# A two-layer encoder trunk in fp32: two of four weight sums made by accumulating transfers, heads turned some steps after their gating, last chunks of output blocks bank by bank

## The chip, the core and the metric

The kernel runs on one core of one Trainium2 chip. The metric is the device time of one execution in microseconds (us), of which several runs were taken and the median is given. The core's engines are named as in the profile: PE (TensorE matmul), PEld (its weight loads), DVE (VectorE), ACT (ScalarE), POOL (GpSimd) and SP (SyncE, which here only issues transfers).

## The reference

Two layers, 512 tokens, model width 2048, all in float32. Each layer normalises its input, projects it with one matrix of 7184 columns, runs two head groups on the columns, and maps the gated result back with a 2048x2048 matrix.

```python
h = rmsnorm(x, g_pre)
z = h @ w_in                                    # 2048 x 7184
gq, gk, gv, gg, ga, aq, ak, av, ag = split_columns(z)
log_a = log_sigmoid(ga @ w_alpha + b_alpha) / 16          # forget gate, rank 16
o_gla = gla_chunk_causal(gq, gk, gv, log_a)     # 4 heads, chunks of 64: S_c = a*S_(c-1) + k_dec^T v; o = q S_c
o_gla = rmsnorm(o_gla, g_gla) * silu(gg)
o_att = chunk_band_attention(aq, ak, av, rel_bias)        # 8 heads of 128, softmax over own and earlier chunks
o_att = rmsnorm(o_att, g_att) * silu(ag)
y = concatenate([o_gla, o_att]) @ w_out         # 2048 x 2048
return x + rmsnorm(y, g_post)
```

## The kernel before

**Products.** A product of two fp32 matrices is made of three matmuls in a rounded format: each operand is split into a high part (the rounded value) and a low part (what is left), and high x high, high x low and low x high are added up in PSUM. Weights are split on the chip. A job of the weight stream is one chunk of 128 partitions by 1024 fp32 (512 KB): `load` is its transfer on SP's queue (line 141, into a tile `raw` or `H`), `high` its cast on ACT (line 183, `wh`), `low` the subtraction on DVE (line 187, `wl = source - wh`). `ahead()` runs after each job and prepares loads up to five jobs ahead, `high` up to four and `low` three. The rings have four tiles `raw`, four `H`, four `wh`, three `wl` and four `sa` (streamed activations).

**Blocks.** A layer's weights are 18 blocks of 512 columns (14 of the input projection, 4 of the output projection). Two input blocks and two output blocks go through `std_gemm`: eight chunks, four PSUM banks, one for each 128 tokens, 24 matmuls of 128x512 for each chunk (line 275). The other blocks go in pairs through `fast_gemm`: a pair of blocks is made by seven half-size products P1, P5, P6, P3, P7, P2, P4 of four chunks each, 28 jobs where plain products would need 32. There are six such pairs of input blocks (`PAIRS[0]` to `PAIRS[5]`) and one of output blocks (`W23`, `end` in the code). `PAIRS[2]` and `PAIRS[3]` hold the attention's q and k and are made feature-major with matmuls of 128x256 (line 339); the rest are token-major with 128x512 (line 349). The products accumulate in two pairs of banks, X and Y, in turn.

**Weight sums.** P5, P6, P7 and P2 need sums of weight quarters. With b0 and b1 the two blocks and top and bottom their halves, P1 loads H = b0 top; P5 loads a `raw` and adds it, H += b1 top (DVE, line 176); P6 the same with b1 bottom (line 176); P7 loads b0 top again and takes raw = H - raw, which is b1 top + b1 bottom (DVE, line 180); P2 loads b0 bottom and adds it to H after the split (line 190). In `W23` the order is P2, P7, P4 and P7 adds two loaded `raw` tiles (line 178).

**Side work.** Everything else (attention heads, forget gate, recurrence, activation sums, norms) is written as Python generators in `tasks`. After each job `Pace` advances them by `rate` steps (`pump`), and so places their instructions between the jobs' instructions. A scheduler then orders each engine's instructions by priority, which follows the order of the code. The steps named below are, with the lines of the kernel before:

- `attend`, two heads a and b in the order of the string `ORDER`: scores (S, three matmuls, lines 718 to 720), transposes of the probabilities (T, 739), product with the values (P, 756), gate (G, DVE line 770 into a tile `sg`), turn (R, four transposes of `sg` on PE, line 781, then a copy on ACT and two splits).
- `forget_gate_decay`: a running sum over tokens by matmuls with a constant triangle (lines 623, 624, 626, 635) of the logarithm of the forget gate, whose high and low parts come from ACT and DVE (`split`, lines 105 and 106).
- GLA units (four for every two heads): `outer` (904, products of decayed keys and values, whose operands are split by lines 105 and 106), `states`, `read` (937), `norm`, `gate` (955), `turn` (965).
- `output_sums`: sums of output activations for `W23` (lines 497 to 506), written to memory as `oS` by POOL's queue (line 492).
- Line 1070 is the eviction of an output block's bank on DVE; line 448 the first normalisation.

PSUM has four banks for the blocks (`mm`) and four for side work (`ax`).

Of the kernel before, what the change touches and what calls it, by code (L numbers as in the profile page):

```python
# [33 lines left out]
def hybrid_trunk(  # L34
# [100 lines left out]
    class Job:  # L135
# [7 lines left out]

        def load(self):
# [7 lines left out]
            elif k == "P5":  # L152
                p["r", c] = self.fetch(rtile("raw"), b1, top)
# [5 lines left out]
            elif k == "P7":  # L159
                p["r", c] = self.fetch(rtile("raw"), b0, top)  # L160
            elif k == "P2":
                p["r", c] = self.fetch(rtile("raw"), b0, bottom)
# [5 lines left out]
        def high(self):  # L168
# [3 lines left out]
            else:  # L172
                h, r = p["H", c], p.get(("r", c))
                src = h if k in ("P1", "P5", "P6", "P4") else r
                if k in ("P5", "P6"):
# [3 lines left out]
                elif k == "P7":  # L179
                    nc.vector.tensor_tensor(out=r, in0=h, in1=r, op=ALU.subtract)  # L180
# [46 lines left out]
    tasks = []  # L227

    def pump(n):
        while n > 0 and tasks:  # L230
            try:
                next(tasks[0])
                n -= 1
            except StopIteration:
                tasks.pop(0)

    def until(cond):
        while not cond():
            assert tasks
            pump(1)  # L240

    def drain():
        while tasks:
# [325 lines left out]
    def layer(l):  # L569
# [42 lines left out]
        def forget_gate_decay():  # L612
# [20 lines left out]
            for t in range(NT):  # L633
# [13 lines left out]
                yield  # L647
                pend.append((t, la, lah, lal))
# [3 lines left out]
            yield  # L652
# [18 lines left out]
        std_gemm(l, AG1, range(NT), CO, operand_in, gate_evac(1, 1), rate=1.3)  # L671
# [33 lines left out]
        class Head:  # L705
# [90 lines left out]
            "- - aS3 aS2 aS1 aS0 aT3 bS3 aT2 aP3 bS2 aT1 aP2 bS1 aT0 aP1 bS0 aP0 aG "  # L796
            "bT3 bT2 bP3 bT1 bP2 aR bT0 bP1 bP0 bG - - - - bR"
        ).split()

        def attend(hd, qk):  # L800
            heads = {"a": Head(hd, qk, 0), "b": Head(hd + 1, qk, 1)}
            for step in ORDER:
# [10 lines left out]
                elif step[1] == "G":  # L813
                    h.gate()
                else:
                    h.turn()
                yield
            heads_done.add(hd)
# [25 lines left out]
        fast_gemm(l, PAIRS[2], qk_consume(0), rate=2, feature_major=True)  # L844
        fast_gemm(l, PAIRS[3], qk_consume(1), rate=2, feature_major=True)
# [33 lines left out]
        fast_gemm(l, PAIRS[4], kq_consume, rate=2)  # L879
# [4 lines left out]
        class Unit:  # L884
# [24 lines left out]
            def states(self):  # L909
                h, p = self.h, self.p  # L910
                self.sg = sgt([2, 256])
# [72 lines left out]
        def gla_heads(j, gvh, gvl):  # L984
# [6 lines left out]

            new(0)
# [3 lines left out]
            for k in range(5):  # L996
# [3 lines left out]
                if k < 4:  # L1000
                    units[k].read()
                    yield
# [3 lines left out]
                if k:  # L1006
                    units[k - 1].turn()
                    yield
                if k < 4:
                    units[k].norm()  # L1010
                    yield
# [183 lines left out]
```

## Time and profile before

| | |
|---|---|
| runs | 1718.1, 1722.27 and 1723.86 us, median 1722.27 |
| the profiled execution | own time 1726.13 us, span in the profile 1724.3 us |
| mean granted TensorE clock | 0.985 |
| PE busy | 1656.8 us, 96% of the span |
| DVE, ACT, POOL busy | 70%, 51%, 12% |
| transfers | 455 MB, 61.8% of 16 DMA engines' span on SP's queue and 11.8% on POOL's |

The span is what the profile covers; the own time of the same execution is 1.8 us longer. A busy share is an average over all stages. In a row of the view of waits stand the waiting engine and line, what ended the wait, the sum of such waits, their number and the longest. In a row of the view of windows stand the stretch, its length, the busy time of each engine with the number of its instructions, the granted clock (PEclk), the share of the DMA engines and GB/s. In a row of the timeline stand start, length, engine, line, operation and, in brackets, the idle time before it and what ended it.

### The profile page before, as it was taken

Reading aid. Unit: us, or ns where it says so; the run is one execution under the profiler, and the core shown is the slowest. Engines: PE = TensorE matmul, PEld = TensorE weight load, DVE = VectorE, ACT = ScalarE, POOL = GpSimd, SP = SyncE. Lnnn points to the kernel's source line nnn. Section 1 sums busy time; section 2 is a strip of 40 time slices with the busy share of each in tenths; the row PEclk is TensorE's granted clock in tenths of the full one; section 3 lists DMA queues with packets and bytes.
Section 4 is the critical chain, followed back from the end, with each engine's and each line's share of the span. In section 5 each row is a group of like instructions: output and inputs, shape, how many; then the busy total and the mean of one; then the engine's idle time right before and its main releaser. Section 6 shows DMA issues by size and latency. Waiting matters only on the chain. (4 is left out here: it accounts for less than half of the span.)

```text
span 1724.3 us, 25039 instructions
## 1 busy us (share of the span) xinstructions
PE 1656.8 (96%) x9090; PEld 1406.6 (82%) x9090; DVE 1214.7 (70%) x1547; ACT 874.0 (51%) x1444; POOL 201.9 (12%) x368
## 2 busy tenths in 40 slices
PE   7999999999999999999999999999999999999896
PEld 5888889999987876778678888899998888667784
DVE  5756877677767777476887567677777677754767
ACT  8634544455665534344584345444556555344443
POOL 0210000011202102110022000000121011021101
PEclk8999999999999999999999999999999999999999
DMA  7986886758847786596769587867686678767964
GB/s 266 344 315 229 330 297 239 278 179 292 296 146 284 245 321 240 199 351 238 244 238 385 211 314 280 314 227 260 199 308 225 205 275 281 278 220 233 371 233 168
DMA packets 143003, 455.05 MB, mean 264 GB/s; under 512 B 15444, under 2 KB 32212, under 8 KB 142880
## 3 DMA queue, kind: packets, MB, share of 16 engines
q1 hardware_dynamic: 119984, 373.76, 61.8%
q0 software_dynamic: 22176, 78.41, 11.8%
q8 instruction: 72, 1.18, 0.3%
q10 hardware_dynamic: 720, 1.28, 0.2%
q14 instruction: 51, 0.42, 0.1%
HBM read 381.28 MB, written 72.11 MB: 263 GB/s over the span
## 5 line engine op out<-in xcount | busy, mean ns | idle before, releaser
L349 PE MATMUL mm<-wh,sa 128*128 128x512 f32 x1536 | 490.0, 393 | 0.5
L183 ACT CAST wh<-raw 128x1024 fp32r<-128x1024 f32 x248 | 261.7, 1056 | 256.8 <-PE mm L349 83.6
L187 DVE TENSOR_TENSOR wl<-raw,wh 128x1024 fp32r<-128x1024 f32 x248 | 300.7, 1219 | 82.8 <-PE mm L275 25.5
L183 ACT CAST wh<-H 128x1024 fp32r<-128x1024 f32 x224 | 235.0, 1051 | 243.8 <-PE mm L349 131.8
L187 DVE TENSOR_TENSOR wl<-H,wh 128x1024 fp32r<-128x1024 f32 x224 | 273.4, 1222 | 105.4 <-PE mm L349 44.7
L349 PEld LDWEIGHTS mm<-wh,sa 128*128 128x128 f32 x1536 | 288.4, 188 | 63.0 <-issue 2.5
L349 PE MATMUL mm<-wl,sa 128*128 128x512 f32 x768 | 301.2, 392 | 7.0 <-DVE wl L187 6.9
L339 PE MATMUL mm<-sa,wh 128*128 128x256 f32 x1280 | 234.1, 284 | 0.0
L349 PE MATMUL mm<-wh,a 128*128 128x512 f32 x576 | 193.4, 406 | 7.4 <-DVE g L1070 7.4
L339 PEld LDWEIGHTS mm<-sa,wh 128*128 128x128 f32 x1280 | 199.5, 192 | 0.2
L339 PE MATMUL mm<-sa,wl 128*128 128x256 f32 x640 | 181.2, 283 | 0.0
L349 PEld LDWEIGHTS mm<-wl,sa 128*128 128x128 f32 x768 | 144.5, 188 | 38.6 <-DVE wl L187 10.2
L275 PE MATMUL mm<-wh,a 128*128 128x512 f32 x512 | 171.9, 395 | 0.1
L349 PEld LDWEIGHTS mm<-wh,a 128*128 128x128 f32 x576 | 111.8, 194 | 33.3 <-DVE g L1070 8.2
L176 DVE TENSOR_TENSOR H<-H,raw 128x1024 f32<-128x1024 f32 x112 | 136.8, 1223 | 2.8
L339 PEld LDWEIGHTS mm<-sa,wl 128*128 128x128 f32 x640 | 122.6, 192 | 0.0
L349 PE MATMUL mm<-wl,a 128*128 128x512 f32 x288 | 115.9, 402 | 0.0
L180 DVE TENSOR_TENSOR raw<-H,raw 128x1024 f32<-128x1024 f32 x48 | 58.8, 1224 | 80.2 <-DMA raw<-in_w_dram 80.1
L275 PEld LDWEIGHTS mm<-wh,a 128*128 128x128 f32 x512 | 96.2, 188 | 21.8 <-issue 1.5
L275 PE MATMUL mm<-wl,a 128*128 128x512 f32 x256 | 101.0, 395 | 2.4 <-DVE wl L187 2.4
L339 PE MATMUL mm<-a,wh 128*128 128x256 f32 x512 | 96.1, 288 | 0.0
L727 POOL TENSOR_SCALAR sm<-sm 128x1 f32<-128x1 f32 x64 | 31.8, 497 | 539.3 <-DVE sm L723 529.4
(191 smaller groups left out, 2415.6 us busy)
## 6 DMA issues: line engine op xcount, KB each, us to landing
raw<-in_w_dram SPq DMA_DIRECT2D x312, 512.0 KB, 5.2
sa<-S SPq DMA_DIRECT2D x192, 512.0 KB, 4.8
H<-in_w_dram SPq DMA_DIRECT2D x56, 512.0 KB, 5.4
sa<-A SPq DMA_DIRECT2D x48, 512.0 KB, 6.1
S<-g POOLq DMA_DIRECT2D x32, 512.0 KB, 7.6
oS<-g POOLq DMA_DIRECT2D x32, 512.0 KB, 7.2
sa<-oS SPq DMA_DIRECT2D x32, 512.0 KB, 4.7
sg<-t POOLq DMA_DIRECT2D x32, 256.0 KB, 5.6
```

What stands on the lines that cost most here:

```text
L176: nc.vector.tensor_tensor(out=h, in0=h, in1=r, op=ALU.add)
L180: nc.vector.tensor_tensor(out=r, in0=h, in1=r, op=ALU.subtract)
L183: last_cast[0] = nc.scalar.copy(self.wh, src).ins
L187: nc.vector.tensor_tensor(out=self.wl, in0=self.src, in1=self.wh.bitcast(F32), op=ALU.subtract)
L275: nc.tensor.matmul(pss[o], a[:, part, t], rhs[:, kk, :], start=(i == 0 and kk == 0 and m == 0), stop=(i == n - 1 and kk == 1 and m == 2),)
L339: nc.tensor.matmul(dst, lhs[:, kk, f], a[:, part, tok], start=(fresh and kk == 0 and m == 0 and ft % 2 == 0), stop=(c == 3 and kk == 1 and ...
L349: nc.tensor.matmul(out_ps[t], a[:, part, tok], rhs[:, kk, :], start=(fresh and kk == 0 and m == 0), stop=(c == 3 and kk == 1 and m == 2), ...
L727: nc.gpsimd.tensor_scalar(out=nmx, in0=mx, scalar1=-1.0, scalar2=None, op0=ALU.mult)
```

## The change

**Sums by transfers.** P5 no longer loads a `raw` tile on SP's queue and adds it on DVE: POOL issues a transfer that adds b1 top from memory to the tile H (`add`, line 145 of the kernel after). P7 of the six input pairs is built in the same way: b1 top is added to the `raw` tile of P6, which holds b1 bottom. P6's sum, P2's sum and P7 of `W23` stay on DVE. Per layer these are 28 and 24 transfers, so 104 in all that move from SP to POOL, and 104 DVE instructions of 128x1024 that fall away (56 of line 176, all 48 of line 180). The bytes read from memory are the same. PE and ACT execute the same instructions.

**Turns later.** A list `delayed` holds functions with a count of steps. A head's turn is put there with 8 steps when its gate is written, a GLA unit's turn with 5. Some empty steps in `ORDER`, in the forget gate and ahead of the GLA units go in or out, and the rates 2 and 1.8 become 2.1 and 1.7. The GLA units' `sg` tiles alternate between two rings.

**Last chunks bank by bank.** `std_gemm` has had an argument `lag`: the last `lag` chunks are done for one bank after the other instead of all banks for each chunk. The second input block (AG1) and the second output block now have lag=2, the first output block lag=1, which with one chunk leaves the order of matmuls as it was.

```diff
+        def add(self, tile_, blk, c):
+            nc.gpsimd.dma_start(tile_, w[self.l, blk, c].rearrange("p (k n) -> p k n", k=2), accum_op=ALU.add)
...
             elif k == "P5":
-                p["r", c] = self.fetch(rtile("raw"), b1, top)
+                self.add(p["H", c], b1, top)
...
             elif k == "P7":
-                p["r", c] = self.fetch(rtile("raw"), b0, top)
+                self.add(p["r", c], b1, top)
...
-                if k in ("P5", "P6"):
+                if k == "P6":
                     nc.vector.tensor_tensor(out=h, in0=h, in1=r, op=ALU.add)
                 elif k == "P7" and ("r2", c) in p:
                     nc.vector.tensor_tensor(out=r, in0=r, in1=p["r2", c], op=ALU.add)
-                elif k == "P7":
-                    nc.vector.tensor_tensor(out=r, in0=h, in1=r, op=ALU.subtract)
...
     def pump(n):
-        while n > 0 and tasks:
-            try:
-                next(tasks[0])
-                n -= 1
-            except StopIteration:
-                tasks.pop(0)
+        while n > 0 and (tasks or delayed):
+            for entry in list(delayed):
+                entry[0] -= 1
+                if entry[0] <= 0:
+                    delayed.remove(entry)
+                    entry[1]()
+            while tasks:
+                try:
+                    next(tasks[0])
+                    break
+                except StopIteration:
+                    tasks.pop(0)
+            n -= 1
...
-        std_gemm(l, AG1, range(NT), CO, operand_in, gate_evac(1, 1), rate=1.3)
+        std_gemm(l, AG1, range(NT), CO, operand_in, gate_evac(1, 1), rate=1.3, lag=2)
...
-            "- - aS3 aS2 aS1 aS0 aT3 bS3 aT2 aP3 bS2 aT1 aP2 bS1 aT0 aP1 bS0 aP0 aG "
+            "aS3 aS2 aS1 aS0 aT3 bS3 aT2 aP3 bS2 aT1 aP2 bS1 aT0 aP1 bS0 aP0 - aG "
...
-                elif step[1] == "G":
+                else:
                     h.gate()
-                else:
-                    h.turn()
+                    delayed.append([8, lambda h=h: turn(h)])
...
-        fast_gemm(l, PAIRS[2], qk_consume(0), rate=2, feature_major=True)
+        fast_gemm(l, PAIRS[2], qk_consume(0), rate=2.1, feature_major=True)
...
                     units[k].gate()
+                delayed.append([5, units[k].turn])
...
-        std_gemm(l, NB_IN, range(NT), OO, operand_out, out_evac(0), rate=1.8)
+        std_gemm(l, NB_IN, range(NT), OO, operand_out, out_evac(0), rate=1.7, lag=1)
...
-        std_gemm(l, NB_IN + 1, range(NT), OO, operand_out, out_evac(1), rate=0.8)
+        std_gemm(l, NB_IN + 1, range(NT), OO, operand_out, out_evac(1), rate=0.8, lag=2)
```

Three places show how the instructions move. The first is PE's order in layer 0 at the first scores of `PAIRS[2]`, in the first chunks of product P2 (`a_48`, `a_56`, `a_64` are the activations of its chunks 0, 1 and 2; `mm` and `ax` are PSUM tiles, `g_496` to `g_499` and `g_472` to `g_475` the heads' q and k). Before:

```order
L339 MATMUL mm_2396<-a_48_351,wl_3020 128x256
L718 MATMUL ax_3151<-g_498_2925,g_496_2923 128x256
L719 MATMUL ax_3151<-g_499_2926,g_496_2923 128x256
L720 MATMUL ax_3151<-g_498_2925,g_497_2924 128x256
L339 MATMUL mm_2395<-a_56_390,wh_3023 128x256 x2
```

After:

```order
L348 MATMUL mm_2363<-a_56_390,wl_3003 128x256
L729 MATMUL ax_3133<-g_474_2877,g_472_2875 128x256
L730 MATMUL ax_3133<-g_475_2878,g_472_2875 128x256
L731 MATMUL ax_3133<-g_474_2877,g_473_2876 128x256
L348 MATMUL mm_2362<-a_64_423,wh_3006 128x256 x2
```

The scores stood ahead of chunk 1 (`a_56`) of the product and now stand behind it, one job later.

The second is DVE's order at the start of `W23` in layer 0, where the banks of the last plain output block are evicted (`g8`, `g11`, `g14`, `g15`, from the four `mm` tiles) while the first chunks of `W23` are split. Before, with the tiles' numbers:

```order
L187 TENSOR_TENSOR wl_1477_7459<-H_1464_7370,wh_1469_7413 128x1024
L176 TENSOR_TENSOR H_1464_7370<-H_1464_7370,raw_1490_7542 128x1024
L106 TENSOR_TENSOR g2_1480_7466<-t2_1474_7420,g2_1480_7466 128x512
L106 TENSOR_TENSOR g3_1481_7477<-t2_1472_7418,g3_1481_7477 128x512
L187 TENSOR_TENSOR wl_1482_7499<-H_1470_7415,wh_1478_7461 128x1024
L176 TENSOR_TENSOR H_1470_7415<-H_1470_7415,raw_1501_7574 128x1024
L1070 TENSOR_TENSOR g8_1403_7111<-mm_1428_7179,t2_1427_7177 128x512
L1070 TENSOR_TENSOR g11_1406_7123<-mm_1429_7180,t2_1427_7177 128x512
L1070 TENSOR_TENSOR g14_1409_7135<-mm_1430_7181,t2_1427_7177 128x512
L187 TENSOR_TENSOR wl_1488_7538<-H_1479_7463,wh_1483_7501 128x1024
L176 TENSOR_TENSOR H_1479_7463<-H_1479_7463,raw_1505_7595 128x1024
L1070 TENSOR_TENSOR g15_1415_7153<-mm_1431_7182,t2_1427_7177 128x512
```

After:

```order
L188 TENSOR_TENSOR wl_1429_7363<-H_1416_7274,wh_1421_7317 128x1024
L106 TENSOR_TENSOR g2_1432_7370<-t2_1426_7324,g2_1432_7370 128x512
L106 TENSOR_TENSOR g3_1433_7381<-t2_1424_7322,g3_1433_7381 128x512
L1088 TENSOR_TENSOR g8_1352_7003<-mm_1380_7083,t2_1379_7081 128x512
L1088 TENSOR_TENSOR g11_1355_7015<-mm_1381_7084,t2_1379_7081 128x512
L1088 TENSOR_TENSOR g14_1361_7039<-mm_1382_7085,t2_1379_7081 128x512
L188 TENSOR_TENSOR wl_1438_7438<-H_1422_7319,wh_1430_7365 128x1024
L188 TENSOR_TENSOR wl_1439_7440<-H_1431_7367,wh_1437_7436 128x1024
L1088 TENSOR_TENSOR g15_1367_7057<-mm_1383_7086,t2_1379_7081 128x512
L188 TENSOR_TENSOR wl_1450_7472<-H_1440_7442,wh_1441_7444 128x1024
```

Two additions into H and the splits of chunks 0 and 1 stood ahead of the first eviction; now only the split of chunk 0 does, and the first three evictions stand ahead of the splits of chunks 1 to 3.

The third is POOL's order at the same place, which is new (`H_7274` is the tile of P5's chunk 0, `H_7319`, `H_7367` and `H_7442` those of its chunks 1 to 3; an `oS` is one sum of output activations):

```order
L501 DMA oS_127<-g_1427_7342 128x1024
L501 DMA oS_135<-g_1428_7353 128x1024
L145 DMA H_7274<-in_w_dram 128x1024
L501 DMA oS_131<-g_1432_7370 128x1024
L501 DMA oS_139<-g_1433_7381 128x1024
L145 DMA H_7319<-in_w_dram 128x1024
L145 DMA H_7367<-in_w_dram 128x1024
L145 DMA H_7442<-in_w_dram 128x1024
```

The sums of `W23`'s P5, which stood on DVE, now stand in POOL's queue behind the writes of the output sums, and each of these waits for its split on DVE.

48 lines of the change are left out of this document (28 added, 20 removed).

## The prediction

> **What bounds the kernel now.** I read the page's totals first, then the waits of PE, the timeline around the longest of them, and stretches of the windows view, which give the granted clock and the load of the DMA engines.
>
> ```profile
> span 1724.3 us, 25039 instructions
> PE 1656.8 (96%) x9090; PEld 1406.6 (82%) x9090; DVE 1214.7 (70%) x1547; ACT 874.0 (51%) x1444; POOL 201.9 (12%) x368
> PEclk8999999999999999999999999999999999999999
> ```
>
> PE is the bound: it is idle for 1724.3 - 1656.8 = 67.5 us, and the change leaves its instructions alone. So the time can only come from that idle time, from the clock after it, or from new waits. Which of PE's waits the change touches is in the view of waits; all but the first come once or twice in either layer, so the sums are over both.
>
> ```profile
> PE mm L349 <- DVE wl L187: 7.9, 7, 2.2
> PE mm L349 <- DVE g L1070: 7.4, 2, 3.8
> PE ax L904 <- ACT g L105: 5.2, 2, 3.2
> PE ax L718 <- ACT g L105: 3.9, 2, 2.0
> PE ax L781 <- DVE sg L770: 3.2, 2, 1.7
> PE ax L965 <- DVE sg L955: 2.5, 4, 0.7
> PE ax L965 <- issue: 1.2, 2, 0.6
> PE ax L623 <- ACT t L105: 2.1, 2, 1.1
> PE ax L624 <- DVE t L106: 1.2, 2, 0.6
> PE ax L904 <- DVE g L106: 1.0, 2, 0.5
> ```
>
> A wait has a second price. The timeline shows four of them, and the windows what clock was granted behind them (PEclk is the third number from the end).
>
> ```profile
> 335.89 0.91 PE L718 MATMUL ax<-g,g 128*128 128x512 f32 x2 [1.93 <-ACT g L105]
> 532.91 0.30 PE L781 MATMUL ax<-cst,sg 128*128 128x128 f32 x1 [1.72 <-DVE sg L770]
> 638.91 0.39 PE L904 MATMUL ax<-g,g 64*128 64x256 f32 x2 [3.16 <-ACT g L105]
> 776.47 0.79 PE L349 MATMUL mm<-wh,a 128*128 128x512 f32 x1 [3.61 <-DVE g L1070]
> ```
>
> ```profile
> core 0: us, PE busy (x) PEld busy (x) DVE busy (x) ACT busy (x) POOL busy (x), PEclk, DMA share, GB/s
> 100.00:150.00 50.00, 50.00 (x222) 41.39 (x222) 29.05 (x25) 19.82 (x23) 2.78 (x5) 1.00 0.66 234
> 155.00:231.00 76.00, 75.93 (x336) 62.56 (x335) 56.64 (x51) 38.33 (x43) 4.31 (x8) 1.00 0.82 302
> 231.00:307.00 76.00, 75.85 (x467) 68.28 (x466) 54.34 (x50) 32.72 (x35) 0.00 (x0) 1.00 0.76 271
> 336.20:339.60 3.40, 3.40 (x14) 3.12 (x13) 2.71 (x6) 1.21 (x2) 0.45 (x2) 0.50 0.79 301
> 476.10:479.50 3.40, 3.40 (x10) 2.62 (x10) 2.66 (x3) 0.78 (x2) 0.00 (x0) 0.50 0.00 0
> 640.00:643.40 3.40, 3.40 (x15) 2.39 (x13) 3.22 (x6) 0.41 (x1) 0.00 (x0) 0.51 0.34 122
> 776.50:779.90 3.40, 3.40 (x8) 2.72 (x9) 3.37 (x4) 0.00 (x0) 0.00 (x0) 0.50 1.01 406
> 1189.50:1192.90 3.40, 3.40 (x14) 3.20 (x14) 2.09 (x5) 1.33 (x4) 0.45 (x2) 0.50 0.77 295
> 1329.50:1332.80 3.30, 3.30 (x9) 2.60 (x8) 2.22 (x3) 0.45 (x2) 0.00 (x0) 0.50 0.00 0
> 1493.30:1496.70 3.40, 3.40 (x13) 1.87 (x12) 3.12 (x6) 0.00 (x0) 0.00 (x0) 0.50 0.58 204
> 1629.90:1633.20 3.30, 3.30 (x9) 2.61 (x8) 3.27 (x5) 0.00 (x0) 0.00 (x0) 0.50 0.99 384
> 533.20:536.60 3.40, 3.40 (x18) 2.75 (x17) 3.23 (x7) 1.88 (x4) 1.07 (x2) 1.00 0.64 228
> ```
>
> At full clock a 128x512 matmul takes 50 / 222 = 0.225 us. In 776.5 to 779.9 PE counts as busy but runs 8 of them, which are 1.8 us of work in 3.4 us: the stretch costs 1.6 us. There are four of them in either layer, behind the scores, the decay sums, GLA's outer products and the start of W23. Behind the head turn's wait of 1.72 us the clock stayed at 1.00, behind the scores' 1.93 us it fell to 0.50.
>
> The Trainium skill, "TensorE: Matmul & The Clock Gate", section "Why this matters for your kernels", asks for no PE-idle gaps over about 3 us, since one window of idle drops the clock. The trace differs: 1.93 us was enough. By the rule only the stalls of 3.16 us and more would carry a stretch, three as far as the rows tell, and the saving below would be 3 x 1.6 = 4.8 us in place of 12.8 us; I go by the rows.
>
> **The change, part by part.** *Later steps and last chunks.* The pairs of 28 jobs in the windows took 76 us, so a job is 2.71 us.
>
> - Scores: one job later, 2.71 us against a wait of 1.93 us; gone, 3.9 us in both layers. Nothing stands between them and the product but matmuls that are ready.
> - Decay sums: two to four empty steps more, at about two steps a job, so 2.7 to 5.4 us against 1.1 and 0.6 us; gone, 2.1 + 1.2 = 3.3 us.
> - Head turns: 8 steps behind the gate are 4 jobs, 10 us, against 1.7 us. The heads of the last pair end in a burst (the code runs steps until they are done, whatever the rate), where I leave 0.5 us; 2.7 of 3.2 us.
> - GLA outer products: four empty steps ahead, 5.4 us against 3.2 + 0.5 us; gone, 5.2 + 1.0 = 6.2 us.
> - GLA turns: all but a layer's last two are covered. In the new order these stand back to back behind the last read with 12 matmuls (2.7 us) between, while norm, POOL's power and the gate run in a row. New wait between 0 and what these turns wait now, (2.5 + 1.2) / 2 = 1.9 us a layer; I take 1.3, nearer to the old, because the chain is the old one; 3.7 - 2.6 = 1.1 us.
> - Start of W23: the wait of 3.61 us is for evictions, and DVE did other things ahead of them:
>
> ```profile
> 770.99 1.23 DVE L176 TENSOR_TENSOR H<-H,raw 128x1024 f32<-128x1024 f32 x1
> 774.59 1.22 DVE L176 TENSOR_TENSOR H<-H,raw 128x1024 f32<-128x1024 f32 x1
> 775.73 1.88 DVE L1070 TENSOR_TENSOR g<-mm,t 128x512 f32<-128x512 f32 x3
> ```
>
> The two additions (2.45 us) go, and with two chunks for each bank the first bank ends three times 6 x 0.225 = 1.35 us, 4.1 us, earlier before the end. Both together are more than 3.61 us; but chunk 7's split is needed 4.1 us earlier, too. I leave 0.8 us a layer (bounds 0 and 2); 7.4 - 1.6 = 5.8 us.
>
> These are 3.9 + 3.3 + 2.7 + 6.2 + 1.1 + 5.8 = 23.0 us. With the stalls of scores, decay, outer and W23's start go eight stretches at half clock, 8 x 1.6 = 12.8 us. If the splits were late at these places for another reason, this cover would be gone and the 12.8 us with it. The first output block's lag of one chunk costs and brings nothing, since its matmuls keep their order.
>
> *Sums by transfers.* The rows for the work that goes and for what is nearest to the new transfers:
>
> ```profile
> L176 DVE TENSOR_TENSOR H<-H,raw 128x1024 f32<-128x1024 f32 x112 | 136.8, 1223 | 2.8
> L180 DVE TENSOR_TENSOR raw<-H,raw 128x1024 f32<-128x1024 f32 x48 | 58.8, 1224 | 80.2 <-DMA raw<-in_w_dram 80.1
> L183 ACT CAST wh<-raw 128x1024 fp32r<-128x1024 f32 x248 | 261.7, 1056 | 256.8 <-PE mm L349 83.6
> raw<-in_w_dram SPq DMA_DIRECT2D x312, 512.0 KB, 5.2
> S<-g POOLq DMA_DIRECT2D x32, 512.0 KB, 7.6
> L492 POOL DMA_DIRECT2D oS<-g x32 | 17.1, 533 | 106.6 <-DVE g L106 105.7 <-issue 0.7
> L727 POOL TENSOR_SCALAR sm<-sm 128x1 f32<-128x1 f32 x64 | 31.8, 497 | 539.3 <-DVE sm L723 529.4
> ```
>
> DVE loses 104 x 1.22 = 127 us, 70% to 63% of the span. By itself that is worth nothing on the path: PE hides DVE's work. It is worth something only where PE waits for DVE: W23's start (counted) and 7.9 us for `wl`, most of it at W23's end, where line 178's sums stay; I count 0 (bounds 0 and 7.9).
>
> SP loses 104 issues, POOL gets 104 of 0.53 us, 55 us, 12% to 15%. What counts is how late a sum lands. Its tile is free when P1's `wl` is made. With three `wl` tiles that is two jobs ahead of P1's matmuls at the latest, and P5's matmuls come four jobs after P1's: 6 x 2.71 = 16.3 us, less `wl` itself (1.22), the cast (1.06) and P5's `wl` (1.22), so 12.8 us from release to landing. P7's chunks have six jobs or more as well. The trace has no transfer that adds. From below: a plain one from memory, 5.2 us. From above: a write by POOL's queue and a load one after the other, 7.6 + 5.2 = 12.8 us, which just fits. I take 9, between a POOL transfer and that bound, so no wait. DVE's 80 us of waits at line 180 come back as waits of ACT for the same landing, which PE does not see.
>
> The load of the DMA engines: 271 GB/s x 76 us are 20.6 MB, 39 chunks, in 0.76 x 76 = 57.8 us, 1.47 us a chunk. Eight sums a pair are in there at the price of a plain load. At twice the price they add 11.8 us, and the share goes from 0.76 and 0.82 to 0.92 and 0.97; at three times to 1.07 and 1.13, and the pair becomes bound by transfers. I take twice or less, no cost, and keep three times as a rival.
>
> The Trainium skill, "Collectives: The Full Stack", section "The bandwidth ceiling: the fold count and why AG ≠ RS ≠ AR", says that an add in the transfer path runs slower because it needs two source reads (measured ratio 1.93 there). By it the sum would be that of the twice-case, without a wait; no run here shows it yet.
>
> At W23's start the sums stand on POOL behind the writes of `oS`, each of which waits for a split on DVE, and behind the sum stands the next write. That takes 2 to 4 us of the 12.8; I put 0.7 us a layer (bounds 0 and 2), 1.4 us. Elsewhere a sum that waits holds up POOL's small steps, such as the negated maxima of line 727, for which the exponential waits. Transposes stand three steps behind their scores, about 4 us; I put 1 us in all (bounds 0 and 8).
>
> **The sum.** 23.0 + 12.8 - 1.4 - 1.0 = 33.4 us. The profiled execution's own 1726.1 us becomes 1692.7. It lies 3.9 us above the median of 1722.3, so the median becomes 1688.9, and with what DVE's relief may add at the small `wl` waits I say 1688. Within 0.3% (5 us) a measurement of this kernel can't tell a change; the three runs shown differ by 5.8 us.
>
> **Rivals.**
>
> - *Sums land late (slower).* The place is P5's and P7's first chunk in each of the 12 input pairs. If a sum needs 16 us from release, each pair waits 16 - 12.8 = 3.2 us and then runs 1.6 us less at half clock: 4.8 x 12 = 58 us against 33 gained, 1747. It decides at (12.8 + 33 / 12 - 1.6), about 14 us. If the engines are bound at three times the price, a pair goes from 76 to between 81 and 86 us: +5 to +10 x 12, 60 to 120 us against 33, 1716 plus up to 90. For it speaks the share of 0.82 in the first pair, with 1.01 at W23's start; against it that 5.2 us landings come at that same load. 0.16 together.
> - *Waits move only partly (faster, less).* The half-clock stretches may come back from waits that take their place (last GLA turns, W23's POOL queue, a burst of scores waiting for banks), or PE waits at P5 for a sum by under a microsecond in some pairs. With the stretches kept, 1688 + 13 = 1701; with half a microsecond more for each pair, 1707. For it speaks how near 1.72 us (no drop) lies to 1.93 us (a drop). 0.25.
> - *Only the longest waits carry a stretch.* If the clock falls only behind waits of 3.16 us and more, and the drops behind the shorter ones have another cause that stays, three stretches go and not eight: 8 us less, 1696. Against it speaks that the drop at 336.20 begins right behind the wait of 1.93 us. 0.05. (This is the rule of the Trainium skill quoted above.)
> - *Nothing comes of it.* The stalls go, and P5's sums take back 1.5 to 2.5 us in each pair: 1716 to 1726, 0.06.
>
> **Numbers.** My forecast, a gain of 28 to 46 us, has 0.48; its own range is 1676 to 1694. Faster by over 0.3%: 0.48 + 0.25 + 0.05 = 0.78; within: 0.06; slower: 0.16. The range goes down to 1676 (0.03 below, if also `wl`'s 7.9 us go) and up to 1718, which leaves out the slower rival and a part of the last.
>
> **What would show it.** Right: no wait of over 0.5 us for scores, decay sums and outer products; PE at 1.00 in all but the start and W23's end; the new transfers landing within 13 us; DMA share under 1 in the first two pairs, and these still 76 us long; ACT's cast waiting for sums in place of line 180. Wrong: PE waiting for `wh` or `wl` at P5 or P7 in every pair; pairs of 80 us and more; a share at 1 throughout. The step that I trust least is the landing time of a sum, for which the trace has no row.

## The result and the profile after

The changed kernel is slower by 0.8%: a median of 1740.2 us of 22 runs against 1726.7 us of 22 runs of the kernel before, ratio 1.0081 with a 95% interval of 1.0061 to 1.0102. The forecast was 1688 us, with a range that ended at 1718. The profiled execution took 1736.2 us, its span is 1734.5 us; before it was 1724.3. The page of the changed kernel:

```profile
span 1734.5 us, 24943 instructions
PE 1659.7 (96%) x9090; PEld 1406.8 (81%) x9090; DVE 1096.7 (63%) x1443; ACT 866.9 (50%) x1444; POOL 283.4 (16%) x472
DMA  7998997868858897598769698987698679866974
q1 hardware_dynamic: 105008, 319.23, 51.5%
q0 software_dynamic: 37152, 132.94, 29.1%
H<-in_w_dram POOLq DMA_DIRECT2D x56, 512.0 KB, 8.3
raw<-in_w_dram POOLq DMA_DIRECT2D x48, 512.0 KB, 7.1
```

DVE lost 118 us (127 were forecast), and PE's idle time went up from 67.5 to 74.8 us. The sums land after 8.3 and 7.1 us in the median, where I had put 9. The queues' rows have the first sign of the price: 54.5 MB moved from SP's queue to POOL's, q1 fell by 10.3 points (61.8 to 51.5) and q0 rose by 17.3 (11.8 to 29.1). PE's waits in the changed kernel:

```profile
PE mm L358 <- DMA sa<-S: 8.2, 4, 4.1
PE mm L358 <- DVE wl L188: 6.7, 6, 2.2
PE ax L729 <- ACT g L105: 4.2, 2, 2.2
PE ax L767 <- ACT t L753: 4.0, 2, 2.2
PE mm L358 <- DVE g L1088: 3.5, 2, 3.2
PE ax L729 <- DVE sm L734: 2.6, 2, 1.3
PE ax L983 <- issue: 2.3, 2, 1.2
PE ax L767 <- DVE t L755: 2.2, 3, 1.5
PE ax L632 <- ACT t L105: 2.0, 2, 1.6
PE ax L633 <- DVE t L106: 1.2, 2, 0.6
```

The outer products' and the head turns' waits are gone. The scores' wait (line 729) is not, although they stand a job later; nor is that of the decay sums (lines 632 and 633, 3.2 us, 3.3 before). And there are new ones: 8.2 us for streamed activations (`sa`, for which PE does not wait in the kernel before), 6.2 us at line 767, the product with the values. The windows of the first two pairs (before: DMA share 0.82 and 0.76) and of the wait for `sa` in layer 0 (616.3 to 620.2, PE stands still):

```profile
core 0: us, PE busy (x) PEld busy (x) DVE busy (x) ACT busy (x) POOL busy (x), PEclk, DMA share, GB/s
155.00:231.00 76.00, 75.97 (x335) 62.30 (x334) 46.36 (x43) 37.32 (x44) 11.40 (x16) 1.00 0.95 302
231.00:307.00 76.00, 76.00 (x467) 68.59 (x466) 46.61 (x42) 33.26 (x36) 6.87 (x8) 1.00 0.88 268
616.30:620.20 3.90, 0.00 (x0) 0.00 (x0) 0.95 (x1) 0.94 (x1) 0.00 (x0) 1.00 1.07 291
```

The same bytes now take 0.13 and 0.12 more of the DMA engines. (A packet counts whole in the stretch in which it starts, so a share can come out a little over 1.) The pairs themselves are as long as before, 76 us, so the forecast's place for a loss, P5 and P7 of every pair, isn't where it arose.

Where it arose is shown by a table of stage lengths, from the first matmul of a block to that of the next, both layers added (us, worked out from the traces):

| | pairs 0, 1 | pair 2 | pairs 3 to 5 | output blocks | W23 | all else | span |
|---|---|---|---|---|---|---|---|
| before | 305.4 | 183.1 | 606.6 | 217.0 | 174.3 | 237.9 | 1724.3 |
| after | 306.3 | 185.6 | 610.3 | 218.8 | 175.1 | 238.4 | 1734.5 |
| after_plain | 304.6 | 179.8 | 585.0 | 220.5 | 172.2 | 238.1 | 1700.2 |
| sums_only | 307.1 | 187.9 | 631.6 | 210.1 | 175.2 | 236.9 | 1748.8 |
| plain_pool | 304.6 | 183.2 | 601.6 | 211.3 | 174.0 | 236.9 | 1711.6 |
| turns_lag | 310.0 | 174.6 | 590.0 | 217.8 | 170.7 | 236.9 | 1700.0 |

The last four are experiments, told next: the changed kernel with transfers that do not add, the sums alone, the sums' transfers alone without the adding, and the moved steps with the last chunks but without the sums. With the adding the changed kernel loses 31 of its 34 us against `after_plain` in pairs 2 to 5, and `sums_only` loses 35 of its 37 us against `plain_pool` there. These are the pairs in which attention, forget gate and recurrence run beside the matmuls.

### The profile page after: what moved, and what is told of

It is laid out like the page before. It is cut to its first block, busy times and chain, and to the rows that moved or that the text cites. A ratio compares the mean times of both kernels' runs of the same rounds, so it can differ in the third digit from the quotient of the medians.

```text
span 1734.5 us, 24943 instructions
## 1 busy us (share of the span) xinstructions
PE 1659.7 (96%) x9090; PEld 1406.8 (81%) x9090; DVE 1096.7 (63%) x1443; ACT 866.9 (50%) x1444; POOL 283.4 (16%) x472
## 3 DMA queue, kind: packets, MB, share of 16 engines
q1 hardware_dynamic: 105008, 319.23, 51.5%
q0 software_dynamic: 37152, 132.94, 29.1%
## 5 line engine op out<-in xcount | busy, mean ns | idle before, releaser
L358 PE MATMUL mm<-wh,sa 128*128 128x512 f32 x1536 | 495.8, 397 | 10.2 <-DMA sa<-S 8.2
L358 PEld LDWEIGHTS mm<-wh,sa 128*128 128x128 f32 x1536 | 292.0, 190 | 77.3 <-DMA sa<-S 9.3
L358 PE MATMUL mm<-wh,a 128*128 128x512 f32 x576 | 185.9, 394 | 3.5 <-DVE g L1088 3.5
L284 PE MATMUL mm<-wh,a 128*128 128x512 f32 x512 | 172.6, 397 | 1.4 <-DVE g L1088 1.2
L191 DVE TENSOR_TENSOR H<-H,raw 128x1024 f32<-128x1024 f32 x56 | 68.3, 1223 | 61.6 <-DMA raw<-in_w_dram 61.3
L145 POOL DMA_DIRECT2D raw<-in_w_dram x48 | 41.9, 874 | 317.3 <-DVE wl L188 248.7
L284 PE MATMUL mm<-wh,g 128*128 128x512 f32 x256 | 87.5, 398 | 1.8 <-ACT t L584 1.8
```

The costliest lines, as they stand in the source:

```text
L145: nc.gpsimd.dma_start(tile_, w[self.l, blk, c].rearrange("p (k n) -> p k n", k=2), accum_op=ALU.add)
L191: nc.vector.tensor_tensor(out=h, in0=h, in1=self.src, op=ALU.add)
L284: nc.tensor.matmul(pss[o], a[:, part, t], rhs[:, kk, :], start=(i == 0 and kk == 0 and m == 0), stop=(i == n - 1 and kk == 1 and m == 2),)
L358: nc.tensor.matmul(out_ps[t], a[:, part, tok], rhs[:, kk, :], start=(fresh and kk == 0 and m == 0), stop=(c == 3 and kk == 1 and m == 2), ...
```

## The experiments

**Parts alone.** The theory S was that the sums are the loss, T that the moved steps are. `sums_only` has the new `add`, its two places (first P5, then P7) and DVE's two operations taken out, and nothing else:

```diff
-                p["r", c] = self.fetch(rtile("raw"), b1, top)
+                self.add(p["H", c], b1, top)
...
-                p["r", c] = self.fetch(rtile("raw"), b0, top)
+                self.add(p["r", c], b1, top)
```

> The kernel before with the 104 accumulating transfers alone (P5 and P7), order of side work and last chunks as before. Theory S (the sums are the loss): P6's raw tile now lives until P7's split, so P2's loads come late and DVE stands in order behind them; the scores' wait grows from 1.9 to over 3 us, the time goes up by 5 to 15 us (ratio 1.003 to 1.009). Theory T (the moved steps are the loss): the sums are nearly free or gain a little, ratio 0.994 to 1.002. Both expect pairs 0 and 1 to stay at about 76 us in spite of a DMA share of 0.88 to 0.95.

Measured: 1753.9 us, ratio 1.0182 (1.0158 to 1.0207). The loss of the sums is 28 us, twice what S had put at most. Pairs 0 and 1 stayed at 76.6 to 76.9 us, as both theories had it.

`turns_only` is the kernel after with these lines undone and the three `lag` arguments taken out.

> The kernel after with P5 and P7 as before (loaded on SP's queue, summed on DVE) and without lag: the moved steps, the empty steps and the rates alone. Theory S: without the late loads the scores, decay sums, head turns and outer products gain what was forecast, 12 to 25 us, ratio 0.985 to 0.993. Theory T: the wait of 4 us for a streamed sa tile in pair 5, behind the fetch of the last heads' turned output, and the waits of the value products in pair 3 are still there, ratio 0.998 to 1.008.

Measured: 1712.2 us, ratio 0.9930 (0.9914 to 0.9947), 14 us faster. T is out: the moved steps gain. One thing got worse, W23's start, which waits longer for its evictions than before (7.4 us in both layers):

```profile
PE mm L360 <- DVE g L1090: 10.2, 2, 5.1
```

`lag_only` has only lag=2 for AG1 and the second output block in the kernel before:

```diff
-        std_gemm(l, AG1, range(NT), CO, operand_in, gate_evac(1, 1), rate=1.3)
+        std_gemm(l, AG1, range(NT), CO, operand_in, gate_evac(1, 1), rate=1.3, lag=2)
...
-        std_gemm(l, NB_IN + 1, range(NT), OO, operand_out, out_evac(1), rate=0.8)
+        std_gemm(l, NB_IN + 1, range(NT), OO, operand_out, out_evac(1), rate=0.8, lag=2)
```

> The kernel before with lag=2 for AG1 and the second output block alone. The wait at W23's start (3.6 and 3.8 us) falls by 2 to 4 us in each layer and the half-clock stretch behind it goes: ratio 0.994 to 0.998. If the two H sums on DVE ahead of the evictions decide, it stays over 2 us and the ratio is 0.998 to 1.001.

Measured: 1725.9 us, ratio 0.9999 (0.9982 to 1.0016): nothing in the time. But the wait did not stay where it was. The row for the evictions is gone, and another has grown, which was 2.4 us before:

```profile
PE mm L275 <- DVE wl L187: 9.8, 5, 4.6
```

It is the second output block that now waits, 3.7 and 4.6 us, for the split of its last chunk (the first matmul with that chunk's `wl`), which the new order needs earlier. So the time of the second forecast came about in another way than it said: the two H sums ahead of the evictions do not decide alone.

`late_fetch` was to move one fetch on SP's queue in the kernel after:

> The kernel after, where the fetch of a pair of heads' turned output (a<-oa) is issued three jobs later, so that the write it waits for has landed and SP does not stand in front of the sa loads. Theory F (SP's queue stands behind this fetch): PE's waits of 4.1 and 3.9 us for sa go, with the half-clock stretches behind them, 10 to 12 us less than after, ratio to before 1.000 to 1.003. Rival: the sa loads are late because the DMA engines are loaded (share 1.07 there); the waits stay over 2 us and the time is within 3 us of after.

Measured: 1738.5 us, ratio 1.0081 (1.0057 to 1.0105). It tells nothing of the theory, since the scheduler put the fetch back at its old place on SP's queue; it is in effect a second measurement of the changed kernel. `late_fetch2` below has it really moved.

**Which sum, and what of it.** `p5_only` and `p7_only` have one of the two lines each.

> The kernel before with P5's 56 accumulating transfers alone; P7 is loaded and subtracted as before. If the cost is that of the transfer itself it is shared by number, 56 of 104: 12 to 17 us over before, ratio 1.007 to 1.010. If it is the raw tiles of P6 held until P7, P5 alone costs under 5 us.

> The kernel before with P7's 48 accumulating transfers alone. If the cost is that of the transfer itself: 10 to 15 us over before. If it is the raw tiles held until P7: 20 us and more, with DVE's waits at P2's sum (line 191) as long as with both sums, near 59 us.

Measured: 1738.3 us, ratio 1.0068 (1.0043 to 1.0092), and 1743.3 us, 1.0083 (1.0051 to 1.0115). Medians 11.6 and 16.6 us over before add up to the 28 of both. By the number of transfers, 56 and 48, it would be 15 and 13; the intervals, 7 to 16 and 9 to 20 us, allow that, and don't tell whether P7's cost more each. DVE's waits at P2's sum did grow to the 59 us expected for P6's raw tiles held longer (58.7 in `p7_only`, 35.8 before), but in `plain_pool`, which holds them as long, they are 39.5 us.

`plain_pool` is `sums_only` without the adding, so that P5's and P7's sums are left out:

```diff
-            nc.gpsimd.dma_start(tile_, w[self.l, blk, c].rearrange("p (k n) -> p k n", k=2), accum_op=ALU.add)
+            nc.gpsimd.dma_start(tile_, w[self.l, blk, c].rearrange("p (k n) -> p k n", k=2))
```

> The kernel before with the 104 transfers of P5 and P7 on POOL's queue in the same places, with the same waits, but overwriting their tile in place of adding to it (this leaves the two sums out; PE, DVE and ACT execute what they do with the sums). Theory A (the adding is the price: more of the DMA engines' time and a later landing): the DMA share of pairs 0 and 1 falls back to 0.82 and 0.76, the landing to 6 or 7 us, and the time to 1715 to 1732. Theory O (the place is the price: POOL's queue, the release of the tile as the start, P6's raw tiles held longer): the time stays at 1745 to 1756.

Measured: 1712.2 us, ratio 0.9908 (0.9877 to 0.9938). This is the run that settles the main point. The same transfers at the same places, with the same bytes and the same releases, and with the same DVE instructions gone, are 14 us faster than before; with the adding they are 28 us slower. The adding costs 42 us by the medians, 47 by the ratios. Of the rows, first `plain_pool`, then `sums_only`:

```profile
q0 software_dynamic: 37152, 132.94, 21.2%
H<-in_w_dram POOLq DMA_DIRECT2D x56, 512.0 KB, 6.0
raw<-in_w_dram POOLq DMA_DIRECT2D x48, 512.0 KB, 4.6
155.00:231.00 76.00, 76.00 (x337) 62.96 (x336) 47.16 (x42) 38.61 (x43) 8.64 (x16) 1.00 0.84 304
ACT wh L184 <- DMA H<-in_w_dram: 15.4, 10, 4.0
ACT wh L184 <- DMA raw<-in_w_dram: 15.0, 8, 3.8
```

```profile
q0 software_dynamic: 37152, 132.94, 28.8%
H<-in_w_dram POOLq DMA_DIRECT2D x56, 512.0 KB, 9.3
raw<-in_w_dram POOLq DMA_DIRECT2D x48, 512.0 KB, 6.9
155.00:231.00 76.00, 75.71 (x335) 62.25 (x334) 46.68 (x42) 37.74 (x43) 11.40 (x16) 1.00 0.94 297
ACT wh L184 <- DMA H<-in_w_dram: 72.9, 34, 6.5
ACT wh L184 <- DMA raw<-in_w_dram: 58.2, 32, 4.3
```

POOL's queue took 11.8% of 1724.3 us before, 203 us of all 16 engines. Plain, it takes 21.2% of 1711.6, 363 us; adding, 28.8% of 1748.8, 504 us. Over 104 transfers that is (363 - 203) / 104 = 1.53 us and (504 - 203) / 104 = 2.89 us for 512 KB: adding takes 1.88 times as long. The Trainium skill gives a ratio of 1.93 in "Collectives: The Full Stack", section "The bandwidth ceiling: the fold count and why AG ≠ RS ≠ AR", for a collective of four ranks that adds against one that copies, and puts it down to two source reads. The ratio here is near it; that a second read is the reason no trace here shows.

`turns_lag` is the kernel after with both sums as before, so `turns_only` with the last chunks bank by bank.

> The kernel after with both sums as before: moved steps and last chunks bank by bank. If lag brings, with the moved steps, what was forecast for W23's start, its waits fall from 5.3 and 5.2 us (moved steps alone) to under 3 us each and the time by 4 to 8 us below the moved steps alone: 1704 to 1709. Rival: lag brings nothing here either, since wl of the last chunk is needed earlier, 1710 to 1714.

Measured: 1705.2 us, ratio 0.9865 (0.9836 to 0.9894), faster than both kernels. Its waits at W23's start fell to 2.4 us in all (the row of line 1090 below). With the moved steps lag brings 7 us, alone it brought nothing: the wait for the split of that last chunk, 8.3 us there, is 1.5 us here. Why it is short here no run shows.

`after_plain` is the changed kernel with plain transfers.

> The whole changed kernel with the same 104 transfers, overwriting in place of adding (leaves P5's and P7's sums out). If the moved steps, the last chunks and the freed DVE bring what the single runs show, 1705 for the first two less 14 for the third, 1688 to 1695, and the adding alone is what turned the change around. If the freed DVE and the moved steps take the same waits away, 1698 to 1706.

Measured: 1702.5 us, ratio 0.9866 (0.9842 to 0.9890). The adding costs 1740.2 - 1702.5 = 38 us here. Of the single waits, those for the scores are still 3.4 us (4.2 with the adding), while those for `sa` are gone (8.2) and those of the decay sums are 0.4 us (3.2). The freed DVE and the transfers' move from SP's queue to POOL's, together worth 14 us in the old order, bring 3 us on top of the moved steps, which is not to be told from nothing. The second forecast, that both take away the same waits, fits.

**How the adding gets at the time.** Theory E: the DMA engines' load makes all transfers land later. Theory L: the sum's own landing is late, and ACT's cast, in order, holds up the side work behind it. A first try, `plain_load`, copied 512 KB beside each plain transfer:

```diff
+            nc.gpsimd.dma_start(junk[0], w[self.l, blk, c])
```

> The kernel with 104 plain transfers on POOL's queue in place of the sums (P5's and P7's sums left out), where each is followed by a copy of the same 512 KB from memory to an unused place in memory. Nothing waits for the copy; it only takes the DMA engines' time, about what the adding takes beside the plain transfer (1.2 to 1.5 us of all 16 engines). Theory E (the engines' load is the price, all transfers land later): 1735 to 1755, as with the sums. Theory L (the later landing of the sum itself is the price, since ACT's cast stands in order behind it): 1712 to 1722, near the plain transfers alone.

Measured: 1814.6 us, ratio 1.0524 (1.0502 to 1.0547), but the copies, for which nothing waits, all ran in the first 350 us. It shows only what a full load does: the first pair of layer 0 took 114 us. It doesn't tell E from L. The window of its first pair:

```profile
155.00:231.00 76.00, 59.40 (x220) 45.05 (x218) 27.21 (x24) 24.10 (x29) 19.06 (x41) 0.89 1.00 393
```

`sums_cast3` and its control have ACT's casts prepared a job later:

```diff
-        for what, n in (("load", 3), ("high", 3), ("low", 3), ("load", 4), ("high", 4), ("load", 5)):
+        for what, n in (("load", 3), ("high", 3), ("low", 3), ("load", 4), ("load", 5)):
```

> The kernel before with both accumulating transfers and the casts on ACT prepared three jobs ahead, not four. Theory L (casts that wait for a sum hold up ACT's side work): a job later the sum has mostly landed, ACT's waits for it fall from 131 us to under 70 and the time falls by 8 us or more below 1754. Theory E: within 4 us of 1754, or slower, since a cast that starts later gives less room.

> The control: the kernel before with the casts prepared three jobs ahead, not four. Theory L and E: nothing waits for it, 1722 to 1732. If the fourth job's cast was needed, PE waits for wh or wl in the pairs and the time goes over 1735.

Measured: 1742.3 us, ratio 1.0110 (1.0085 to 1.0135), and the control 1713.5 us, ratio 0.9940 (0.9917 to 0.9964). Both gain 11.6 and 11.5 us, the control as much, so it is no sign for L; ACT's waits for the sums were still 135 us (131 without the edit), in a profiled execution that with 1753.1 us was the slowest of its six. That the control gained was expected by neither theory, and why it did was not followed up.

`adds_dram` has the load without the landing, `plain_late` the landing without the load. In both a copy of one column of an earlier `wl` holds POOL's queue until that is made. These are lines of `adds_dram`; `plain_late` has 3 in place of 4 and issues the plain transfer into the tile:

```diff
+            ins = nc.gpsimd.tensor_copy(probe, stream[self.i - 4].wl.bitcast(F32)[:, 0, 0:1]).ins
+            with tc.issue_after(ins):
...
+                nc.gpsimd.dma_start(junk[0][:, :, :512], w[self.l, blk, c].rearrange("p (k n) -> p k n", k=2), accum_op=ALU.add)
```

> The kernel before with 104 accumulating transfers of the same bytes, issued by POOL each when the wl four jobs ahead is made (a copy of one column of it holds POOL until then), but into memory that nothing reads; P5's and P7's sums are left out, so that no cast waits for a landing. Theory E (the engines' load is the price): DMA share in pairs 0 and 1 near 0.94 and 0.90, and 1740 to 1760. Theory L (the sum's own landing is the price): 1708 to 1720.

> The 104 plain transfers of before (no adding, P5's and P7's sums left out), each held back on POOL until the wl three jobs ahead is made, about one job (2.7 us) later than its tile is free at P5; the landing then comes about as late as that of the adding ones (9 us after the release), at the engines' load of plain ones. Theory L: ACT's waits for these tiles grow from 30 us to over 100 and the time from 1712 to 1735 or more. Theory E: 1710 to 1722.

Measured: 1760.8 us, ratio 1.0210 (1.0177 to 1.0244), and 1737.4 us, ratio 1.0054 (1.0025 to 1.0082). The load by itself costs all that the sums do and more. Its sums go to memory, have more packets (50464 against 37152 on that queue) and take 3.10 us of all engines by the sum above, not 2.89, and it loses 10 us against `plain_pool` in pairs 0 and 1 too, where the sums lose 2; in pairs 2 to 5 it loses 36 us, the sums 35. The lateness costs, too, about 25 us over `plain_pool` by the ratios ((1.0054 - 0.9908) x 1726.7), but with more waiting than the sums cause; its rows:

```profile
ACT wh L187 <- DMA raw<-in_w_dram: 125.3, 53, 6.2
ACT wh L187 <- DMA H<-in_w_dram: 85.6, 40, 6.8
```

That is 211 us against the sums' 131. POOL, in order, stands 304 and 371 us at the copies of the two runs, no longer than at the tiles' release in `plain_pool` (395 us), and ACT's waits for POOL's negated maxima are 49.9 and 49.4 us, less than there (57.7); so POOL's queue doesn't show as the cause. So E can make up the price by itself and L is real; how the 42 us divide between them these runs don't settle.

How full the engines are doesn't tell the stages apart. Cut into stretches of 5 us, so many of them have a DMA share of 1 or more (worked out from the packets in the traces; in brackets the mean share):

| | pairs 0, 1 | pairs 2 to 5 |
|---|---|---|
| before | 14% (0.79) | 7% (0.71) |
| plain_pool | 21% (0.80) | 14% (0.73) |
| sums_only | 48% (0.92) | 27% (0.79) |

Full stretches are more frequent in pairs 0 and 1, which lose 2 us, than in pairs 2 to 5, which lose 35. What pairs 2 to 5 have besides is side work that waits for transfers. PE's waits at the decay sums, the scores and the product with the values (lines 624, 719 and 757) are 29.8 us in `sums_only` and 13.8 in `plain_pool`, those for `sa` 6.4 and 0.4 us, and stretches of 3.4 us at half clock are 13 and 6.

One place in `sums_only` shows a way from load to PE, the decay sums of layer 0. Before, a load of the attention bias was issued at 466.73 and let DVE go on at 472.37; here the same load, issued at 478.07, took until 488.05. First its rows from the timeline, then the window while it was under way, then the row and the window of before, last those of `plain_pool`, where the load was issued at 466.3:

```profile
478.07 0.33 SPq L699 DMA_DIRECT2D bias<-in_rel_dram  x1
488.05 0.11 DVE L700 MEMSET bias<- 64x64 f32 x1 [8.48 <-DMA bias<-in_rel_dram]
490.00 0.62 ACT L105 CAST t<-t 128x512 fp32r<-128x512 f32 x1 [4.75 <-DVE t L642]
490.67 0.79 PE L624 MATMUL ax<-t,later 128*128 128x512 f32 x1 [6.29 <-ACT t L105]
```

```profile
478.00:488.00 10.00, 6.39 (x28) 4.91 (x27) 1.36 (x4) 4.84 (x9) 1.32 (x3) 0.96 1.07 250
```

```profile
472.37 0.11 DVE L699 MEMSET bias<- 64x64 f32 x1 [1.33 <-DMA bias<-in_rel_dram]
466.70:472.40 5.70, 5.70 (x27) 4.61 (x25) 3.71 (x6) 4.42 (x9) 2.11 (x2) 1.00 0.92 357
```

```profile
472.62 0.11 DVE L700 MEMSET bias<- 64x64 f32 x1 [4.85 <-PE mm L350]
475.24 0.50 PE L624 MATMUL ax<-t,later 128*128 128x512 f32 x1 [2.65 <-ACT t L105]
466.30:472.50 6.20, 6.20 (x28) 4.85 (x26) 1.31 (x2) 3.66 (x9) 1.01 (x3) 1.00 0.99 396
```

The engines are full (1.07) while they move 250 GB/s; before they moved 357 GB/s at 0.92, with plain transfers 396 at 0.99. A 256 KB load takes 10.0 us and not 5.6, DVE stands in order behind it for 8.48 us, ACT waits for DVE's result, and PE waits 6.29 us for ACT where it had waited 1.02 us (473.73 in the trace of before). Not all of that is the adding: in `plain_pool` the load takes 6.2 us, but DVE, which has fewer sums to make, comes to it early and stands 4.85 us (the row names PE, but the load lands at 472.5), and PE waits 2.65. The adding's part here is 3.6 us of the 6.29.

**The fetch and the fastest version.** `late_fetch2` lets the fetch of heads 4 and 5 wait for the end of product P2, not P1, and ties it to the last `sa` load issued by then:

```diff
-                if ("P1", 3) in passed and 2 * i in heads_done and (0, i) not in op_att:
+                if ("P1" if i in (0, 1, 3) else "P2", 3) in passed and 2 * i in heads_done and (0, i) not in op_att:
...
+                    with tc.issue_after(last_sa[0]):
+                        nc.sync.dma_start(flat(op_att[0, i]), oa_d[l][0, i])
```

> The kernel after, where the one fetch (a<-oa, of heads 4 and 5's turned output) that waits for its write stands on SP's queue behind the last sa load of pair 5. Theory F (SP's queue stands behind this fetch): PE's waits of 4.1 and 3.9 us for sa go, with the half-clock stretches behind them: 8 to 12 us less than after, 1728 to 1733, ratio 1.001 to 1.004. Theory E (the DMA engines' load): the waits stay over 2 us each, within 4 us of after (1740).

Measured: 1735.5 us, ratio 1.0064 (1.0041 to 1.0086), which overlaps with the changed kernel's interval and lies between the two forecasts. The two long waits went, but PE still waits 8.8 us for `sa`, now in ten pieces:

```profile
PE mm L359 <- DMA sa<-S: 8.8, 10, 2.2
```

The order of SP's queue decides where the wait falls; that there is one goes, in this order of steps, with the adding, since `after_plain` has none. It is not the adding alone that can make it: `turns_lag`, without a single such transfer, waits 6.3 us for `sa`.

`turns_cast3` joins `turns_lag` and the later casts; `best_fetch` adds the moved fetch.

> The kernel after with both sums as before (moved steps and last chunks) and the casts on ACT prepared three jobs ahead. If the two gains (21 us and 11 us) come from different waits: 1690 to 1698. If they are the same waits of side work: 1700 to 1708.

> Both sums as before, moved steps, last chunks, casts three jobs ahead, and the same fetch behind the last sa load. At the plain load this wait is 1.5 us in all here: 1695 to 1702, not to be told from the version without it (1701).

Measured: 1700.7 us, ratio 0.9861 (0.9831 to 0.9892), and 1706.6 us, ratio 0.9902 (0.9879 to 0.9924). The later casts bring nothing that can be told on top of the moved steps (0.9865), and the moved fetch nothing either. In both traces the wait for the split of the second output block's last chunk is back, 9.6 and 9.1 us against 1.5 in `turns_lag`. The versions to keep are `turns_lag` and `turns_cast3`, 1.4% faster than before.

## Why the prediction was wrong

- *Moved steps and last chunks, forecast 23.0 + 12.8 = 35.8 us.* The mechanism held, the size was less: `turns_lag` gains 21.6 us by the medians, 18 to 28 by the interval. In the traces PE's idle time falls from 67.5 to 56.5 us, 11.0 of the 23.0 forecast. Its waits:

```profile
PE mm L360 <- DVE wl L190: 7.7, 8, 2.2
PE mm L360 <- DMA sa<-S: 6.3, 4, 2.2
PE ax L769 <- DVE t L757: 3.7, 4, 1.5
PE mm L360 <- DVE g L1090: 2.4, 2, 1.8
PE ax L985 <- issue: 2.3, 2, 1.2
PE ax L731 <- DVE sm L736: 2.1, 2, 1.1
```

  The scores' wait for their split, the decay sums' and the outer products' are gone, as the terms of 3.9, 3.3 and 6.2 us had it, and so are the head turns'. The GLA turns wait 2.3 us in all, where I left 2.6. W23's start waits 2.4 us, where I left 1.6. What I hadn't counted are new waits of the later steps, 6.3 us for `sa`, 3.7 at the product with the values, 2.1 at a score that waits for a bank. They are 12.1 us, 0.9 of which stood at the product with the values before: nearly all of the 12.0 us that are missing in the idle time. At W23's start the prediction named what lag can cost, the last chunk's split needed earlier; alone it cost about all that lag brought (`lag_only`).
- *Half clock.* This term held. Apart from its start and end, the execution before has ten stretches at half clock: the eight of the forecast and two more, at 848.2 and 892.5, which it left out. `turns_lag` has two, at 623.9 and 1675.2. PE's busy time, in which such stretches count, fell by 13.3 us (1656.8 to 1643.5) against 12.8 forecast. In the changed kernel there are nine, one of them twice as long, behind the waits that stayed or are new.
- *Sums by transfers, forecast 0 for the adding, 1.4 and 1.0 us beside it.* This is the step that failed: 38 us were measured for the adding (`after` against `after_plain`). The sizes that went into it held: I put 0.92 and 0.97 as the DMA share at twice the price and 0.88 and 0.95 were measured, 9 us to landing and 8.3 and 7.1 were measured. The conclusion "twice or less, no cost" was wrong. It compared the mean share of a stage with 1 and the landing with the need of the sum's own product, and both hold in pairs 0 and 1, from which I took the rows: they are 76 to 77 us long. They hold in pairs 2 to 5 as well, where the mean share is only 0.79 in `sums_only`, and yet these lose 35 us: there the extra 1.4 us of engine time for each sum meets loads and casts for which the side work waits, and PE waits for the side work. The prediction had no term for that; how much of it is the load and how much the sums' own late landing stays open.
- *"DVE's 80 us of waits at line 180 come back as waits of ACT for the same landing, which PE does not see."* They came back, 131 us in `sums_only`, but ACT's queue also carries the exponentials, copies and splits of the side work, and PE waits for those: `plain_late`, which has such waits and no load, loses 25 us to `plain_pool`.
- *DVE's relief, forecast 0.* With the transfers' move to POOL's queue, from which no run separates it, 14 us in the old order, about 3 in the new one, so that 0 was right here within the noise.
- *The rivals.* "Sums land late" had the sign and 0.16 of the chance, but the wrong place: it looked for PE's waits at P5 and P7 of every pair, and required three times the price for bound engines. Less than twice was enough, without pairs bound by transfers. Two sums among the rivals are off: 60 to 120 us against 33 gained would end at 1749 to 1809, not at "1716 plus up to 90", and 1.5 to 2.5 us back in each of the 14 pairs would be 1709 to 1723, not 1716 to 1726. The Trainium skill ("TensorE: Matmul & The Clock Gate", section "Why this matters for your kernels") asks for no gaps over about 3 us. Shorter ones were enough here too: `turns_lag` has a stretch at a clock of 0.53 behind a wait of 2.2 us for `sa`.

```profile
623.70:627.10 3.40, 3.16 (x8) 2.52 (x9) 2.43 (x3) 0.66 (x1) 0.00 (x0) 0.53 1.03 414
```

## What to carry to other kernels

Price an adding transfer at nearly two plain ones (1.88 here), and don't hold that against a stage's mean share of the DMA engines alone: pairs at a mean of 0.92 lost next to nothing and pairs at 0.79 lost 35 us. Ask which side work waits for a transfer and which engine in order stands behind it. A transfer that lands in time for its own consumer can still delay others, and along such a chain the delay reaches the bound engine. Work taken off an engine that isn't the bound (118 us of DVE here) pays only for waits that nothing else takes away; to find which of two edits pays, run each alone and run the transfer without its adding. And look at the waits even when the time doesn't change: one can have taken the other's place, as in `lag_only`.

## What was not expected of the hardware

An adding transfer is longer to issue as well: POOL's instruction for it takes 0.89 us, for a plain one of the same tile 0.54 us (first `sums_only`, then `plain_pool`; minimum, median and maximum in ns):

```profile
L145 POOL DMA_DIRECT2D H<-in_w_dram x56: 852/890/939, 111.4 to 1658.9; - x56
```

```profile
L145 POOL DMA_DIRECT2D H<-in_w_dram x56: 530/541/622, 111.6 to 1623.1; - x56
```

And a wait of the same length at the same place, 1.75 us after and 1.76 us before at the gates of AG1 in layer 1, was followed by half clock in the changed kernel and not in the kernel before (first after, then before):

```profile
931.80:935.20 3.40, 3.40 (x10) 2.61 (x9) 1.52 (x3) 1.15 (x2) 1.21 (x3) 0.50 1.03 417
```

```profile
926.60:930.00 3.40, 3.40 (x16) 2.74 (x16) 1.85 (x4) 1.24 (x2) 1.47 (x3) 1.00 1.03 422
```

So the length of a wait doesn't decide alone near 1.75 us whether the clock falls. That this is part of why the runs of a kernel spread by 15 us and more was not tested.
